# Skip weights loaded as one contiguous row and picked apart by two copies, and a new order of the steps in the output's last four quarters

## The chip, the cores and the metric

The kernel runs on one core of a Trainium2 chip. The metric is device time in microseconds (us) for one execution. Before the change it is 1481.93 us, the median of three runs (1481.75 to 1485.11).

## The reference, cut to what matters

Two layers work on 1024 tokens of width 1024. The first mixes tokens in chunks of 128 by a masked matrix per group (spatial gating); the second is a Mamba-2 scan with 32 heads of 64 channels, whose output gets a skip term. A final RMSNorm closes the program.

```python
h = x
for i in range(2):
    hn = rmsnorm(h, norm_w[i])
    h = h + (spatial_gating_mixer if i == 0 else ssd_mixer)(hn, ...)
return rmsnorm(h, final_norm_w)

# in ssd_mixer: one skip weight per head, d_skip has 32 numbers
y = y_diag + y_off + x * d_skip.reshape(G, J)[..., None]
```

## The kernel before, in words

**Products.** Every large product is a blocked one with seven block products in place of eight. Its float32 operands are split into a high part, a cast on ScalarE (ACT), and a low part, a subtraction on VectorE (DVE); the helper `split` (L111, L112) does this, and `mm3` (L134 to L136) makes three matmuls of the parts. The halves of the weights lie in rotating buffers `wh` and `wl`, three of each. All instructions are written out by hand in program order for each engine; each engine works through its own list in that order and waits where an operand is missing.

**The first layer's wide products.** `head` and then `rest` (L886) compute the gate path `v` for eight groups in two wide blocks, A and B. The object `Wide` has `prep` (ACT cast `wh`, DVE rest `wl`), `mm`, `keep` (ACT copies an accumulator to `u`) and `out`: DVE adds the accumulator and `u` into a tile `vt` (L396) and a DMA stores it in `v_d` (L397). Four buffers of the tag `k2` hold the `vt` tiles. The second block's `C11` is stored through the DMA queue of GpSimd (POOL); the stores around it go through SyncE's queue (SP).

**The mixing matrices.** Among the products of `rest` lie `mix_b`, in which TensorE (PE) transposes the masked matrices `ws` (L869) and ACT copies the result to two tiles `wc` (L871), and `mix_c`, in which PE multiplies `wc` by a matrix of ones (L877) and DVE makes `ab` of it (L882). The `wc` tiles are `k2` tiles too: they take the buffers of the first two `vt` tiles of `C11`, so ACT can write them once the DMAs that store these have landed. Product 6 runs around `mix_b`; L877 stands on PE between products 6 and 7.

**The small constants.** Between `head` and `rest` (L829 to L840) SP loads `dt_bias` and `a_log` into `hv`, and the skip weights into `dsk`: partition p of `dsk` needs, in column c, the weight of head 2c for p below 64 and of head 2c + 1 above. The load does this itself, in two DMAs, each with every second number of `d_skip` as source and 64 partitions as target. `dsk` is first used on DVE at L2024, in the second layer.

**The end.** The second layer's output product, the object `Out` called `bo`, ends with block product 3, cut in four units of 128 tokens (`last_mm`, 24 matmuls each). For a unit, `prep_unit` makes the halves `wh` and `wl` of its operand `ya`; `post(3, i)` adds the accumulator to the residual row `u` on DVE (L1232) and ACT squares it (L1251); `rstd_a` adds the two halves' sums on DVE (L1265) and raises them to the power of -1/2 on POOL (L141); `rstd_b` refines this on DVE (L148, L152, L153); `finish_b` scales the left half of the row on ACT (L2201) and the right half on DVE (L2203) and stores both (L2202, L2204), from SP but for the very last left half, which goes from ACT. The left halves were already multiplied by the final norm's weight (`weigh_left`, L2209). The upper four tiles of 128 tokens, `(1, tt)`, have their norm from `rstd_half` in one go before the last product; the lower four, `(0, tt)`, get theirs one by one as their units end.

Of the kernel before, what the change touches and what calls it, by code (L numbers as in the profile page):

```python
# [8 lines left out]
F32 = mybir.dt.float32  # L9
F32R = mybir.dt.float32r  # L10
AF = mybir.ActivationFunctionType
ALU = mybir.AluOpType
# [3 lines left out]
P = 128  # L16
# [13 lines left out]
def kernel(  # L30
# [21 lines left out]
    nc = tc.nc  # L52
    x = x[0]
    out = out[0]
# [3 lines left out]
    cst = ctx.enter_context(tc.tile_pool(name="cst", bufs=1))  # L58
# [12 lines left out]
    def k2(shape, name, dt=F32):  # L71
        return sb.tile(shape, dt, name=name, tag="k2", bufs=4)
# [755 lines left out]
    with tc.manual_schedule():  # L828
        second = head()  # L829
        hv = cst.tile([P, 4], F32, name="hv")  # L830
        nc.sync.dma_start(out=hv[0:32, 0:1], in_=b_dt_bias[0].rearrange("(h o) -> h o", o=1))
        for q in range(4):
            nc.sync.dma_start(out=hv[q * 32:(q + 1) * 32, 1:2], in_=b_a_log[0].rearrange("(h o) -> h o", o=1))
        dsk = cst.tile([P, 16], F32, name="dsk")
        dskv = b_d_skip[0].rearrange("(c f) -> f c", f=2)
        for f in range(2):
            nc.sync.dma_start(out=dsk[f * 64:(f + 1) * 64, :], in_=dskv[f].partition_broadcast(64))
        nA = hv[:, 2:3]
        nc.scalar.activation(nA, hv[:, 1:2], AF.Exp)
        nc.vector.tensor_scalar(nA, nA, -1.0, None, ALU.mult)  # L840
# [1279 lines left out]
    def accs_b(n):  # L2120
        if n == 1:
# [3 lines left out]
    bo = Out(gd, b_w_out, gscale, lambda t, nb: h1_d[t][:, nb * 512:(nb + 1) * 512], accs_b, False,  # L2125
             (1, 2, 7, 6, 4, 5, 3))
    end = {}
# [68 lines left out]
            if c == 3:  # L2196
                bo.prep_unit(0)

    def finish_b(th, tt, rs):
        l, r = bo.row(th, tt, 0), bo.row(th, tt, 1)  # L2200
        nc.scalar.activation(l, l, AF.Identity, scale=rs)  # L2201
        (nc.scalar if (th, tt) == (0, 3) else nc.sync).dma_start(out=outr[th * 4 + tt][:, 0:512], in_=l)  # L2202
        nc.vector.scalar_tensor_tensor(r, r, rs, end["fnwb"][:, 512:], ALU.mult, ALU.mult)  # L2203
        nc.sync.dma_start(out=outr[th * 4 + tt][:, 512:], in_=r)  # L2204

    def weigh_left(th, t0):
        for tt in range(t0, t0 + 2):
            r = bo.row(th, tt, 0)
            nc.vector.tensor_tensor(out=r, in0=r, in1=end["fnwb"][:, 0:512], op=ALU.mult)  # L2209
# [221 lines left out]
    def into_end():  # L2431
        for n in (2, 7, 6, 4, 5):
            for _ in bo.product(n, hook_b):
                pass
        bo.prep_unit(1)
        weigh_left(1, 2)
        r1 = bo.rstd_half(1)
        for tt in range(4):
            bo.last_mm(tt)
            if 0 < tt < 3:  # L2440
                bo.prep_unit(tt + 1)
            if tt:
                bo.post(3, tt - 1)
                bo.rstd_a(0, tt - 1)
            finish_b(1, tt, r1[:, tt:tt + 1])
            if tt:
                finish_b(0, tt - 1, bo.rstd_b(0, tt - 1))
        bo.post(3, 3)
        bo.rstd_a(0, 3)
        finish_b(0, 3, bo.rstd_b(0, 3))  # L2450

    with tc.manual_schedule():
        scans()
        into_end()
# [28 lines left out]
```

## Time and profile before

| What | us |
|---|---|
| median of three runs | 1481.93 |
| the profiled execution's own time | 1481.93 |
| its span in the profile | 1480.2 |
| PE busy in the span | 1452.0 |
| DVE busy | 1041.8 |
| ACT busy | 784.1 |
| POOL busy | 404.5 |

The profile is of one execution. Its span leaves out 1.73 us of the execution's own time, and that time is the median of the runs. A line of the timeline has the start, the duration, the engine, the line in the code, the operation, what it writes and reads, how often it is repeated and, in brackets, how long the engine had stood idle before it and what ended the wait. PEld is the load of weights into PE, which runs beside matmuls. A busy time of PE is not PE at its peak, so the granted clock, which a table by windows gives as PEclk (1.00 is full), is read with it.

### The profile page before, as it was taken

How to read it: one execution, taken by the hardware profiler on the slowest of the kernel's cores; microseconds unless marked ns; L12 is line 12 of the kernel's file. 1: busy time of each engine (PE TensorE's matmuls, PEld its weight loads, DVE VectorE, ACT ScalarE, POOL GpSimd, SP SyncE). 2: the span in 40 equal slices, each digit the busy share in tenths (PEclk: the TensorE clock that was granted, in tenths of full speed). 3: DMA queues.
4: the chain of work that ended last, by engine and by line, in shares of the span. 5: the costliest groups of instructions: out<-in, count | busy, mean ns of one | idle time of the engine just before them, and what ended most of it. 6: DMA issues, size and time to landing. Idle time of an engine off the chain costs nothing. (4 is left out here: it accounts for less than half of the span.)

```text
span 1480.2 us, 20005 instructions
## 1 busy us (share of the span) xinstructions
PE 1452.0 (98%) x7202; PEld 1196.5 (81%) x7202; DVE 1041.8 (70%) x1713; ACT 784.1 (53%) x1261; POOL 404.5 (27%) x451
## 2 busy tenths in 40 slices
PE   9998999999999999999999999999999999999997
PEld 7786888888888888887788888888888888787875
DVE  7864666776666655678665558767787777788976
ACT  7632333222323445565665646657677766866463
POOL 2101110000000023202122323205676767742221
PEclk9999999999999999999999999999999999999999
DMA  8653423332322999957467988786777566699963
GB/s 287 128 171 91 165 91 120 105 120 94 116 85 78 341 265 252 258 132 175 120 159 169 197 163 162 156 248 158 203 185 201 176 190 141 192 282 282 271 115 114
DMA packets 174549, 257.52 MB, mean 174 GB/s; under 512 B 16513, under 2 KB 98673, under 8 KB 171250
## 3 DMA queue, kind: packets, MB, share of 16 engines
q1 hardware_dynamic: 124128, 171.55, 37.7%
q0 software_dynamic: 42688, 70.79, 24.2%
q10 hardware_dynamic: 7634, 13.90, 2.6%
q8 instruction: 57, 0.93, 0.3%
q14 instruction: 42, 0.34, 0.1%
HBM read 187.19 MB, written 51.18 MB: 161 GB/s over the span
## 5 line engine op out<-in xcount | busy, mean ns | idle before, releaser
L134 PE MATMUL acc<-hh,wh 128*128 128x512 f32 x868 | 339.7, 391 | 0.7 <-ACT u L297 0.7
L136 PE MATMUL acc<-hh,wl 128*128 128x512 f32 x868 | 338.3, 390 | 0.4 <-DVE wl L112 0.3
L135 PE MATMUL acc<-hl,wh 128*128 128x512 f32 x868 | 337.8, 389 | 0.0
L136 PEld LDWEIGHTS acc<-hh,wl 128*128 128x128 f32 x868 | 162.9, 188 | 35.7 <-DVE wl L112 1.6
L134 PEld LDWEIGHTS acc<-hh,wh 128*128 128x128 f32 x868 | 163.1, 188 | 34.3 <-ACT u L297 1.1
L135 PEld LDWEIGHTS acc<-hl,wh 128*128 128x128 f32 x868 | 163.0, 188 | 33.0
L112 DVE TENSOR_TENSOR wl<-wr,wh 128x1024 fp32r<-128x1024 f32 (+1 forms) x81 | 96.2, 1188 | 105.8 <-ACT wh L111 105.6
L111 ACT CAST wh<-wr 128x1024 fp32r<-128x1024 f32 (+1 forms) x97 | 99.3, 1025 | 78.7 <-PE acc L135 58.7
L297 ACT COPY u<-acc 128x512 f32<-128x512 f32 x93 | 53.9, 582 | 148.0 <-PE acc L136 147.9
L134 PE MATMUL ab<-hh,wh 128*128 128x512 f32 x288 | 122.2, 424 | 0.0
L136 PE MATMUL ab<-hh,wl 128*128 128x512 f32 x288 | 113.2, 393 | 0.0
L135 PE MATMUL ab<-hl,wh 128*128 128x512 f32 x288 | 112.5, 391 | 0.6 <-DVE hl L112 0.6
L134 PE MATMUL acc<-wh,hh 128*128 128x512 f32 x216 | 85.6, 396 | 0.3 <-DVE vt L396 0.3
L135 PE MATMUL acc<-wl,hh 128*128 128x512 f32 x216 | 84.3, 390 | 1.0 <-DVE wl L364 1.0
L136 PE MATMUL acc<-wh,hl 128*128 128x512 f32 x216 | 84.1, 389 | 0.0
L976 POOL DMA_DIRECT2D y_d<-y x8 | 4.4, 550 | 287.2 <-DVE y L973 287.2
L1949 ACT ACTIVATE wl<-wl,tk 128x128 f32<-128x128 f32 x256 | 81.6, 392 | 0.3 <-DMA wl<-cs_d 0.2
L1967 DVE TENSOR_TENSOR wl<-wl,cw 128x512 f32<-128x512 f32 x64 | 61.0, 965 | 16.2 <-ACT wl L1951 15.1
L112 DVE TENSOR_TENSOR xl<-ya,xh 128x1024 fp32r<-128x1024 f32 x36 | 44.8, 1243 | 37.6 <-ACT xh L111 32.4
L1162 PE MATMUL bo<-wl,xh 128*128 128x512 f32 x192 | 64.2, 392 | 1.3 <-DVE stats L1253 0.7
L134 PEld LDWEIGHTS ab<-hh,wh 128*128 128x128 f32 x288 | 54.4, 189 | 13.3 <-issue 5.7
L111 ACT CAST xh<-ya 128x1024 fp32r<-128x1024 f32 x36 | 37.7, 1048 | 49.8 <-PE ao L1162 35.0
(331 smaller groups left out, 3236.4 us busy)
## 6 DMA issues: line engine op xcount, KB each, us to landing
wr<-in_a_w_in_dram SPq DMA_DIRECT2D x32, 512.0 KB, 3.6
wl<-cs_d SPq DMA_DIRECT2D x64, 256.0 KB, 5.4
wr<-in_b_w_in_dram SPq DMA_DIRECT2D x30, 512.0 KB, 4.3
wb<-in_a_w_out_dram SPq DMA_DIRECT2D x10, 1024.0 KB
wb<-in_b_w_out_dram SPq DMA_DIRECT2D x10, 1024.0 KB, 9.4
wr<-in_b_w_in_dram SPq DMA_DIRECT2D x36, 256.0 KB, 5.3
wide<-in_a_w_in_dram SPq DMA_DIRECT2D x16, 512.0 KB, 7.3
v<-v_d SPq DMA_DIRECT2D x8, 1024.0 KB
```

Of the source, the lines that this page charges most:

```text
L111: nc.scalar.copy(out=hi, in_=src)
L112: return (eng or nc.vector).tensor_tensor(out=lo, in0=src, in1=hi.bitcast(F32), op=ALU.subtract)
L134: nc.tensor.matmul(out=o, lhsT=l[0], rhs=r[0], start=start, stop=False, **kw)
L135: nc.tensor.matmul(out=o, lhsT=l[0], rhs=r[1], start=False, stop=False, **kw)
L136: nc.tensor.matmul(out=o, lhsT=l[1], rhs=r[0], start=False, stop=stop, **kw)
L297: nc.scalar.copy(out=self.u[n][:, i], in_=a)
L976: store = lambda: nc.gpsimd.dma_start(out=y_d[-1], in_=y)
L1162: nc.tensor.matmul(out=o[i], lhsT=X[x_][:, k, i * P:(i + 1) * P], rhs=Y[y_][:, k, :], start=not more and c == 0 and k == 0 and x_ == y_, s ...
L1949: nc.scalar.activation(wl[:, j, :], wl[:, j, :], AF.Relu, scale=-1.0, bias=tokc(2, c, self.g)[:, j:j + 1])
L1967: V.tensor_tensor(out=wl, in0=wl, in1=self.cw[c][:, 640:768].unsqueeze(1).broadcast_to([P, 4, P]), op=ALU.mult)
```

## The change

The two DMAs that pick every second skip weight become one DMA, which copies the 32 numbers as they lie in memory to each of 128 partitions, and two DVE copies that pick every second column out of that tile into `dsk`. In the output's last four units the same steps are put in another order, and one of them is taken in two: for the very last right half, the multiplication by the final norm's weight is made ahead of the norm, into a tile `left`, and only the scaling by the norm follows.

```diff
+        skip = cst.tile([P, 16, 2], F32, name="skip")
+        nc.sync.dma_start(out=skip.rearrange("p c f -> p (c f)"), in_=b_d_skip[0].partition_broadcast(P))
         dsk = cst.tile([P, 16], F32, name="dsk")
-        dskv = b_d_skip[0].rearrange("(c f) -> f c", f=2)
         for f in range(2):
-            nc.sync.dma_start(out=dsk[f * 64:(f + 1) * 64, :], in_=dskv[f].partition_broadcast(64))
+            nc.vector.tensor_copy(out=dsk[f * 64:(f + 1) * 64, :], in_=skip[f * 64:(f + 1) * 64, :, f])
...
-    def finish_b(th, tt, rs):
+    def finish_b(th, tt, rs, weighed=None):
...
-        nc.vector.scalar_tensor_tensor(r, r, rs, end["fnwb"][:, 512:], ALU.mult, ALU.mult)
+        if weighed is None:
+            nc.vector.scalar_tensor_tensor(r, r, rs, end["fnwb"][:, 512:], ALU.mult, ALU.mult)
+        else:
+            nc.vector.tensor_scalar(r, weighed, rs, None, ALU.mult)
...
-        for tt in range(4):
-            bo.last_mm(tt)
-            if 0 < tt < 3:
-                bo.prep_unit(tt + 1)
-            if tt:
-                bo.post(3, tt - 1)
-                bo.rstd_a(0, tt - 1)
-            finish_b(1, tt, r1[:, tt:tt + 1])
-            if tt:
-                finish_b(0, tt - 1, bo.rstd_b(0, tt - 1))
+        bo.last_mm(0)
+        bo.prep_unit(2)
+        bo.last_mm(1)
+        bo.post(3, 0)
+        bo.rstd_a(0, 0)
+        finish_b(1, 0, r1[:, 0:1])
+        bo.prep_unit(3)
+        finish_b(0, 0, bo.rstd_b(0, 0))
+        bo.last_mm(2)
+        bo.post(3, 1)
+        finish_b(1, 1, r1[:, 1:2])
+        bo.rstd_a(0, 1)
+        finish_b(1, 2, r1[:, 2:3])
+        finish_b(0, 1, bo.rstd_b(0, 1))
+        bo.last_mm(3)
+        bo.post(3, 2)
+        bo.rstd_a(0, 2)
+        finish_b(1, 3, r1[:, 3:4])
+        finish_b(0, 2, bo.rstd_b(0, 2))
         bo.post(3, 3)
+        left = k2([P, 512], "left")
+        nc.vector.tensor_tensor(out=left, in0=bo.row(0, 3, 1), in1=end["fnwb"][:, 512:], op=ALU.mult)
         bo.rstd_a(0, 3)
-        finish_b(0, 3, bo.rstd_b(0, 3))
+        finish_b(0, 3, bo.rstd_b(0, 3), left)
```

In the changed file the lines stand one further down from L838 on; the multiplication of a right half, L2203, is L2205 there, and its store, L2204, is L2208. These are SP's DMAs between `head` and `rest`, before:

```order
L397 DMA v_d_79<-vt 256x1x256
L831 DMA hv<-in_b_dt_bias_dram 32x1
L833 DMA hv<-in_b_a_log_dram 32x1 x4
L837 DMA dsk<-in_b_d_skip_dram 64x16x1 x2
L937 DMA v<-v_d_78 128x2048
```

And the same place on SP with the change:

```order
L397 DMA v_d_79<-vt 256x1x256
L831 DMA hv<-in_b_dt_bias_dram 32x1
L833 DMA hv<-in_b_a_log_dram 32x1 x4
L835 DMA skip<-in_b_d_skip_dram 128x32
L938 DMA v<-v_d_78 128x2048
```

Two DMAs with an innermost step of one number (64 partitions by 16 by 1) became one with rows of 32 numbers. DVE at the same place, where the `vt` tiles of `C11` are made, before:

```order
L396 TENSOR_TENSOR vt<-acc,u 128x512
L404 BN_STATS stats<-vt 128x6
L840 TENSOR_SCALAR hv<-hv 128x1
L404 BN_STATS stats<-vt 128x6
L396 TENSOR_TENSOR vt<-acc,u 128x512
```

And with the change:

```order
L396 TENSOR_TENSOR vt<-acc,u 128x512
L404 BN_STATS stats<-vt 128x6 x2
L838 COPY dsk<-skip 64x16 x2
L841 TENSOR_SCALAR hv<-hv 128x1
L396 TENSOR_TENSOR vt<-acc,u 128x512
```

The two copies, which wait for the new DMA, stand between the second and the third `vt` tile of `C11`. The third place is DVE's list in the last product, from the norm of the upper four tiles (`rh`) to the second unit's addition, before:

```order
L153 TENSOR_TENSOR rh<-rr,ru 128x4
L2203 SCALAR_TENSOR_TENSOR u<-u,rh,fnwb 128x512
L112 TENSOR_TENSOR wl<-ya,wh 128x512 x2
L1232 TENSOR_TENSOR u<-bo,u 128x512
L1265 SCALAR_TENSOR_TENSOR stats<-stats 128x1
L2203 SCALAR_TENSOR_TENSOR u<-u,rh,fnwb 128x512
L148 SCALAR_TENSOR_TENSOR ru<-rr,stats 128x1
L152 TENSOR_SCALAR ru<-ru 128x1
L153 TENSOR_TENSOR stats<-rr,ru 128x1
L2203 SCALAR_TENSOR_TENSOR u<-u,stats,fnwb 128x512
L112 TENSOR_TENSOR wl<-ya,wh 128x512 x2
L1232 TENSOR_TENSOR u<-bo,u 128x512
```

And with the change:

```order
L153 TENSOR_TENSOR rh<-rr,ru 128x4
L112 TENSOR_TENSOR wl<-ya,wh 128x512 x2
L1233 TENSOR_TENSOR u<-bo,u 128x512
L1266 SCALAR_TENSOR_TENSOR stats<-stats 128x1
L2205 SCALAR_TENSOR_TENSOR u<-u,rh,fnwb 128x512
L112 TENSOR_TENSOR wl<-ya,wh 128x512 x2
L148 SCALAR_TENSOR_TENSOR ru<-rr,stats 128x1
L152 TENSOR_SCALAR ru<-ru 128x1
L153 TENSOR_TENSOR stats<-rr,ru 128x1
L2205 SCALAR_TENSOR_TENSOR u<-u,stats,fnwb 128x512
L1233 TENSOR_TENSOR u<-bo,u 128x512
L2205 SCALAR_TENSOR_TENSOR u<-u,rh,fnwb 128x512
```

The operand of unit 2 now comes first and the first upper right half behind the first addition; the operand of unit 3 stands between the sum of unit 0 (L1266) and the refinement of its root (L148); one upper half has moved behind the second addition. On ACT the casts for unit 2 now follow those for unit 1 without an upper left half between them. PE's list and POOL's list are the same in both kernels.

## The prediction

> **What bounds the kernel now.** I read the first part of the page, then the waits of PE, the longest first.
>
> ```profile
> PE 1452.0 (98%) x7202; PEld 1196.5 (81%) x7202; DVE 1041.8 (70%) x1713; ACT 784.1 (53%) x1261; POOL 404.5 (27%) x451
> ...
> PE tp L877 <- ACT wc L871: 6.8, 1, 6.8
> PE nw L451 <- POOL ident masks.py:199: 1.4, 1, 1.4
> ```
>
> PE bounds the kernel: 1452.0 of the span's 1480.2 us, so only 28.2 us are idle. One wait, for the two `wc` tiles, is 6.8 us, and the next longest 1.4. The rest of the idle time must lie at the ends. So I looked at two places: around L877, and behind PE's last matmul. First L877, with PE's and ACT's timelines there and the granted clock in two windows:
>
> ```profile
> 133.16 0.39 PE L136 MATMUL acc<-wh,hl 128*128 128x512 f32 x1
> 140.39 3.73 PE L877 MATMUL tp<-wc,ones 128*128 128x512 f32 x4 [6.84 <-ACT wc L871]
> 144.19 0.40 PE L135 MATMUL acc<-wl,hh 128*128 128x512 f32 x1
> 144.43 0.39 PE L136 MATMUL acc<-wh,hl 128*128 128x512 f32 x1
> ...
> 139.75 1.23 ACT L871 COPY wc<-tp 128x512 f32<-128x512 f32 x2 [20.62 <-DMA v_d<-vt]
> ...
> 136.00:137.00 1.00, 0.00 (x0) 0.00 (x0) 0.00 (x0) 0.00 (x0) 0.00 (x0) 1.00 0.05 0
> 142.40:143.40 1.00, 1.00 (x4) 0.48 (x2) 0.79 (x1) 1.00 (x4) 0.00 (x0) 0.50 0.73 270
> ```
>
> PE waits for ACT, and ACT has waited 20.62 us for the DMA that stores a `vt` tile and so frees the buffer of the first `wc`. The wait costs more than itself: the granted clock (third number from the right) falls from 1.00 to 0.50 during it, and L877 and the matmul behind it still run at half. Why is that store late? Here are the stores from POOL in the stretch from 115 to 160 us, the same line's from 160 to 200, the DMAs of the skip weights, and what the queues moved between 117.2 and 139.2 us:
>
> ```profile
> L397 POOL DMA_DIRECT2D v_d<-vt x4: 690/701/729, 119.6 to 123.8; - x4
> DMA to landing us min/median/max: 17.9/19.1/20.0
> ...
> L397 POOL DMA_DIRECT2D v_d<-vt x12: 682/690/702, 162.7 to 189.8; - x12
> DMA to landing us min/median/max: 2.6/2.7/5.0
> ...
> L837 SPq DMA_DIRECT2D dsk<-in_b_d_skip_dram x2: 672/680/687, 117.4 to 118.1; - x2
> ...
> DMA  1000000000000000000000000000000000004799
> q0 software_dynamic: 186, 0.65, 7.7%
> q1 hardware_dynamic: 2230, 0.01, 4.5%
> hv<-in_b_a_log_dram SPq DMA_DIRECT2D x4, 0.1 KB, 2.1
> ```
>
> The four stores take 18 to 20 us to land, the next twelve of the same size 2.6 to 5.0. In between SP's queue (q1) moves 2230 packets that together hold 0.01 MB, and POOL's queue (q0) moves nothing until slice 37 of 40, which is 137 us. The tiny packets are the skip weights: two DMAs of 64 times 16 single numbers are 2048. They come at 2230 / 22 = 101 per us while the transfer engines are 4.5% busy: some 20 us of making descriptors, not of moving data, from 117.4 to about 138.
>
> The second place is the end. These are DVE's rows around its first and last additions there, and PE's last matmul:
>
> ```profile
> 1455.85 0.75 DVE L2203 SCALAR_TENSOR_TENSOR u<-u,rh,fnwb 128x512 f32<-128x512 f32 x1
> 1457.12 1.30 DVE L112 TENSOR_TENSOR wl<-ya,wh 128x512 fp32r<-128x512 f32 x2 [0.52 <-ACT wh L111]
> 1458.33 0.68 DVE L1232 TENSOR_TENSOR u<-bo,u 128x512 f32<-128x512 f32 x1
> ...
> 1464.24 0.68 DVE L1232 TENSOR_TENSOR u<-bo,u 128x512 f32<-128x512 f32 x1
> 1468.35 0.68 DVE L1232 TENSOR_TENSOR u<-bo,u 128x512 f32<-128x512 f32 x1
> 1471.78 0.75 DVE L2203 SCALAR_TENSOR_TENSOR u<-u,stats,fnwb 128x512 f32<-128x512 f32 x1
> 1472.45 0.68 DVE L1232 TENSOR_TENSOR u<-bo,u 128x512 f32<-128x512 f32 x1
> 1473.98 0.16 DVE L1265 SCALAR_TENSOR_TENSOR stats<-stats 128x1 f32<-128x1 f32 x1 [0.85 <-ACT junk L1251]
> 1474.86 0.22 DVE L148 SCALAR_TENSOR_TENSOR ru<-rr,stats 128x1 f32<-128x1 f32 x1 [0.72 <-POOL rr L141]
> 1475.50 0.75 DVE L2203 SCALAR_TENSOR_TENSOR u<-u,stats,fnwb 128x512 f32<-128x512 f32 x1
> ...
> 1469.86 0.39 PE L136 MATMUL bo<-yh,wl 128*128 128x512 f32 x1
> 1475.49 0.72 ACT L2201 ACTIVATE u<-u,stats 128x512 f32<-128x512 f32 x1 [1.55 <-DVE stats L153]
> ```
>
> PE is done at 1470.25, but DVE adds the last unit only at 1472.45: here DVE's list is late by 2.2 us, and everything behind that addition follows in a chain.
>
> **The change part by part.** *The load.* Two DMAs of 2048 single numbers go; one of 128 rows of 128 bytes comes. At 101 packets per us, 128 packets and a few for completion need about 1.4 us, and a small load lands 2.1 us after its issue (the `hv` row): issued at 117.4, it should be there at about 121. POOL's stores, issued from 119.6 on, then take the 2.6 to 5.0 us of the other twelve; the two that `wc` needs land by 126 at worst.
>
> Then `wc` waits only for its transposes, which stand in PE's list one half product ahead of L877:
>
> ```profile
> 127.06 1.03 PE L869 MATMUL tp<-ident,ws 128*128 128x128 f32 x8
> ...
> 1011.63 0.59 PE L1986 MATMUL os<-cw 128*128 128x256 f32 x2
> 1012.07 0.61 PE L1995 MATMUL os<-xbc,state 128*128 128x128 f32 x4
> ```
>
> They end at 128.1; two copies (1.23) give 129.3. PE comes to L877 at 133.39 (133.16 and one step of 0.23, the distance of the matmuls at 144.19 and 144.43), so 4 us of slack cover the copies. Nothing cools the clock then. What L877 takes at full clock is not in the trace, since it runs once. The nearest row is L1986: two passes over 256 columns in 1012.07 - 1011.63 = 0.44, so a pass over 512 takes 0.44 and L877's four 1.76. The second matmul of product 7 then starts at 133.39 + 1.76 + 0.23 = 135.38 in place of 144.19: 8.8 us earlier. The bounds: 6.8 if L877 gains nothing from the clock; 8.8 is also the upper end, as no step is left to shorten. I take 8.8, since the clock was 1.00 until the wait.
>
> What is late next? DVE's low part for product 7's second half: `keep` behind 133.6, a cast of 1.05, a subtraction of 1.22, so 136.5 against 135.1 plus 24 matmuls, 140.6. The loads of the first layer that follow are issued when their buffers are freed, so they move along with PE, and no wait of PE behind this place is over 1.4 us. I take the whole gain as kept.
>
> The Trainium skill, "DMA: Bandwidth & Descriptors", section "Queues, rings and completion order", speaks against this: each transfer engine takes turns between its queues, packet by packet. By that rule POOL's stores need not wait for the end of SP's tiny packets, their lateness has another cause and stays, and this term would be 0. The trace differs: no q0 data until the tiny packets run out.
>
> *The copies.* DVE gets two copies of 64 by 16 between the second and third `vt` tile of `C11`, at about 121.4 (the row of L840 starts at 121.05). The nearest rows are a copy of 128 by 3 and one of 128 by 256, so 0.16 to 0.42 each, and I take 0.2:
>
> ```profile
> L1709 DVE COPY halo<-acc 128x3 f32<-128x3 f32 x8 | 1.3, 156 | 4.9 <-PE acc L136 4.9
> L2011 DVE COPY state<-os 128x256 f32<-128x256 f32 x8 | 3.3, 415 | 0.7 <-POOL ze L2037 0.7
> 141.97 1.22 DVE L364 TENSOR_TENSOR wl<-wide,wh 128x1024 fp32r<-128x1024 f32 x1 [15.43 <-ACT wh L360]
> ```
>
> DVE stands idle 15.43 us soon after, so this costs nothing. The copies also wait for the load, and behind them stand two `vt` tiles, two subtractions and then the low part for product 7: as long as the load lands by 127 or so, DVE reaches that part before ACT's cast is there.
>
> *The order at the end.* Until the first addition DVE now has only the pair of subtractions for unit 2 (1457.12 to 1458.33, 1.21), whose casts no longer wait for the norm: 1455.85 + 1.21 = 1457.06, 1.27 earlier than 1458.33. The distance to the second addition was 5.91, with the pair for unit 3 behind the scaling. Now the pair lies in the wait for POOL's root. Three rows of ACT give when it can start:
>
> ```profile
> 1456.48 1.12 ACT L111 CAST wh<-ya 128x512 fp32r<-128x512 f32 x2
> 1459.11 0.63 ACT L1251 ACTIVATE junk<-u 128x512 bf16<-128x512 f32 x1 [1.50 <-DVE u L1232]
> 1459.74 0.71 ACT L2201 ACTIVATE u<-u,rh 128x512 f32<-128x512 f32 x1
> ```
>
> After an addition come 0.78 to the square (1458.33 to 1459.11), 0.63 to the upper left half, about as much to the cast, and 0.64 to the subtraction (1456.48 to 1457.12): 2.68. The pair takes 1.21, root and scaling 0.64 (1474.86 to 1475.50) and 0.67 (1471.78 to 1472.45): 5.20, so 0.71 less. The other two distances, 4.11 and 4.10, keep their parts: an upper half before the sum lies within the 0.85 us that DVE waits for the square. The last addition comes at 1472.45 - 1.27 - 0.71 = 1470.47, just behind PE's 1470.25, which is the floor (2.2). From there the chain is the same; `left` (0.68) hides in that 0.85 us. The last right half becomes a multiplication with one tensor, which may take less than the 0.75 of now, but the left half on ACT still takes 0.72 beside it, so I count 0. If the early casts help nothing, 0.7 is left. This term: 2.0, between 0.7 and 2.2.
>
> The sum: 8.8 + 2.0 = 10.8 off the profiled execution, whose own time of 1481.93 is the median too: 1471.1 us.
>
> **The rivals.** *The stores are late for another reason.* They are the first on POOL's queue after a long pause, and the rule above says that queues share. Then only the end gains: 1481.93 - 2.0 = 1479.9. Against it: the twelve later stores land early all the same, and q0's start at 137 meets q1's reckoned end at about 138. Chance 0.09.
>
> *A new wait takes part of it.* `wc` is on time, but ACT or DVE hold product 7 or 4, or a transfer that was covered by the pause is late. Half of the 8.8 would go: 1475.5, with a spread from 1473 to 1478. For it: between L877 and product 4's low part DVE has sixteen small operations of the mixing matrices and two subtractions of 1.2 us, and I know their slack only roughly. Chance 0.11.
>
> *Slower: the new load is cut in single numbers too.* Its 128 by 32 numbers would be 4096 packets, 40 us at 101 per us, landing near 158. DVE's copies wait for it, and with them two `vt` tiles with their statistics, two subtractions and product 7's low part (some 6 us of DVE work): PE would start product 7 at 164 in place of 143, so about 21 - 2.0 = 19 us slower, 1501. It decides from the point where the load lands later than about 139. Against it: its rows are contiguous on both sides. Chance 0.03.
>
> **How the numbers follow.** My forecast has the rest, 0.77. A measurement of this kernel tells about 0.3%, 4.4 us, from no change. Faster by more: 0.77 and most of the second rival, 0.87. Within 0.3%: the first rival and a little of the second, 0.10. Slower: 0.03. The range: the terms' lower bounds give 1481.93 - 6.8 - 0.7 = 1474.4, the upper ones 1470.9; with the second rival, and some 2 us below for what the clock or the final stores may give beyond that, 1469.0 to 1476.5.
>
> **What would show it right or wrong.** Right: no wait at L877, a clock of 1.00 from 130 to 145 us, POOL's four stores landing in 2.6 to 5.0, some 2000 packets fewer on q1, and the last addition some 0.2 us behind PE's last matmul. Wrong: the stores still late with the tiny packets gone, a new wait of PE between 133 and 200 us, DVE idle before its two copies, or a last addition more than 1 us behind PE.

## The result, and the profile after

The changed kernel takes 1470.74 us, the median of five runs (1468.51 to 1472.28), against 1481.93 of before, run beside it (five runs, 1481.41 to 1485.11). The ratio is 0.9919, with a 95% interval from 0.9904 to 0.9933: 11.2 us less, where 10.8 had been predicted (1471.1). The profiled execution of the changed kernel is the slowest of its five: 1472.28, span 1470.6.

The first part of its page, and the waits of PE, the longest first:

```profile
PE 1450.5 (99%) x7202; PEld 1196.8 (81%) x7202; DVE 1043.3 (71%) x1716; ACT 783.9 (53%) x1261; POOL 404.0 (27%) x451
...
PE os L1996 <- DVE state L2014: 1.5, 1, 1.5
PE nw L451 <- POOL ident masks.py:199: 1.4, 1, 1.4
```

The wait for `wc` has left the list, and the longest wait is now 1.5 us. Here are PE's and ACT's timelines at the same place (the lines stand one further down than before), and the granted clock in the two windows that were shown of before:

```profile
133.34 0.40 PE L136 MATMUL acc<-wh,hl 128*128 128x512 f32 x1
133.58 1.88 PE L878 MATMUL tp<-wc,ones 128*128 128x512 f32 x4
134.90 0.79 PE L134 MATMUL acc<-wh,hh 128*128 128x512 f32 x1
135.53 0.40 PE L135 MATMUL acc<-wl,hh 128*128 128x512 f32 x1
...
127.86 1.07 ACT L872 COPY wc<-tp 128x512 f32<-128x512 f32 x2 [8.23 <-PE tp L870]
...
136.00:137.00 1.00, 1.00 (x6) 0.83 (x5) 1.00 (x3) 0.00 (x0) 0.00 (x0) 1.00 0.00 0
142.40:143.40 1.00, 1.00 (x6) 0.84 (x5) 0.96 (x2) 1.00 (x2) 0.00 (x0) 1.00 1.00 414
```

ACT now waits for PE's transposes, no longer for a DMA, and copies `wc` 4.7 us before PE gets there. From the last matmul of product 6 to the second of product 7 it is 135.53 - 133.34 = 2.19 us; before it was 144.19 - 133.16 = 11.03. I call this **the stretch** below; it has become 8.84 us shorter. The clock stays at 1.00. This is the line of POOL's stores (the four of `C11` and four later ones) from 115 to 160 us, and the DMA issues from 117.2 to 139.2 us:

```profile
DMA to landing us min/median/max: 2.6/2.8/5.0
...
v_d<-vt POOLq DMA_DIRECT2D x4, 256.0 KB, 2.6
wcT_d<-wc POOLq DMA_DIRECT2D x2, 256.0 KB, 4.1
skip<-in_b_d_skip_dram SPq DMA_DIRECT2D x1, 16.0 KB, 2.8
```

The four stores of `C11` land in 2.6 to 2.7 us (the 5.0 belongs to a later store), where it had been 18 to 20. At the end, DVE's rows from the first addition to the last right half, and PE's last matmul:

```profile
1450.03 0.68 DVE L1233 TENSOR_TENSOR u<-bo,u 128x512 f32<-128x512 f32 x1
...
1455.20 0.68 DVE L1233 TENSOR_TENSOR u<-bo,u 128x512 f32<-128x512 f32 x1
...
1459.31 0.69 DVE L1233 TENSOR_TENSOR u<-bo,u 128x512 f32<-128x512 f32 x1
...
1463.40 0.69 DVE L1233 TENSOR_TENSOR u<-bo,u 128x512 f32<-128x512 f32 x1
1464.12 0.69 DVE L2463 TENSOR_TENSOR left<-u,fnwb 128x512 f32<-128x512 f32 x1
...
1466.45 0.49 DVE L2207 TENSOR_SCALAR u<-left,stats 128x512 f32<-128x512 f32 x1
...
1462.96 0.39 PE L136 MATMUL bo<-yh,wl 128*128 128x512 f32 x1
```

PE is done at 1463.35, and the last addition follows 0.05 us behind, where it had been 2.20. So the 9.6 us between the two spans come together like this: PE's last matmul is 6.90 earlier (1469.86 - 1462.96), the last addition has moved 2.15 nearer to it, and from there to the end of the span it is 7.20 instead of 7.75. Of the 8.84 us won at the stretch this one pair of executions keeps 6.90 at PE's end; whether that loss belongs to the change is one of the questions below.

### The profile page after: what moved, and what is told of

Its sections match the earlier page's. It is cut to its first block, busy times and chain, and to the rows that moved or that the text cites. A ratio compares the mean times of both kernels' runs of the same rounds, so it can differ in the third digit from the quotient of the medians.

```text
span 1470.6 us, 20006 instructions
## 1 busy us (share of the span) xinstructions
PE 1450.5 (99%) x7202; PEld 1196.8 (81%) x7202; DVE 1043.3 (71%) x1716; ACT 783.9 (53%) x1261; POOL 404.0 (27%) x451
```

## The experiments

Two theories stood at the start. The **theory** is the prediction's: the single numbers of the skip weights hold back POOL's stores, and apart from that the end gains some 2 us of its own. The **rivals**: the stores are late for another reason, and the end gains nothing by itself. The line numbers of an experiment differ by a few from those of before.

### The two parts alone

One kernel has the new load and the old end, the other the old load and the new end (`left` included).

The load alone, against before:

```diff
+        skip = cst.tile([P, 16, 2], F32, name="skip")
+        nc.sync.dma_start(out=skip.rearrange("p c f -> p (c f)"), in_=b_d_skip[0].partition_broadcast(P))
...
-            nc.sync.dma_start(out=dsk[f * 64:(f + 1) * 64, :], in_=dskv[f].partition_broadcast(64))
+            nc.vector.tensor_copy(out=dsk[f * 64:(f + 1) * 64, :], in_=skip[f * 64:(f + 1) * 64, :, f])
```

The order alone, against the changed kernel:

```diff
...
-            nc.vector.tensor_copy(out=dsk[f * 64:(f + 1) * 64, :], in_=skip[f * 64:(f + 1) * 64, :, f])
+            nc.sync.dma_start(out=dsk[f * 64:(f + 1) * 64, :], in_=dskv[f].partition_broadcast(64))
```

> Only the load changes; the order at the end is that of before. Theory (tiny packets hold POOL's stores, wc and PE): no wait at L877's matmul, four stores landing in 2.6 to 5.0 us, 8.8 us less than before, 1473.1 if the scan gives nothing back; 1474.9 if the 1.8 us that the profiled run of after lost in the scan come with every early start. Rival (stores late for another reason): the 6.8 us wait stays, 1481.9. In all cases the last addition lies about 2.2 us behind PE's last matmul.

> Only the order at the end changes, left included; the skip weights come as single numbers. Theory (DVE's list was late by 2.2 us): the last addition falls within 0.3 us of PE's last matmul, 2.0 us less than before by the prediction, 1479.9; 2.5 less, 1479.4, if the 0.55 us between last addition and end is saved too. Rival (the end gains nothing of its own, and the shorter end of after came with the early start): 1481.9. The wait of 6.8 us at L877's line stays in both.

On one chip, with 15 runs of before at 1482.42 us (1480.71 to 1484.49): the load alone took 1473.04 (five runs, 1472.48 to 1473.75), ratio 0.9937 with an interval from 0.9924 to 0.9949, so 7.6 to 11.3 us less. The order alone took 1480.29 (eleven runs, 1477.49 to 1482.80), ratio 0.9983, from 0.9974 to 0.9992, so 1.2 to 3.9 us less. The stretch is 2.19 us with the load alone and 11.17 with the order alone. Here are the last addition and PE's last matmul, first of the load alone, then of the order alone:

```profile
1464.49 0.69 DVE L1233 TENSOR_TENSOR u<-bo,u 128x512 f32<-128x512 f32 x1
...
1461.90 0.39 PE L136 MATMUL bo<-yh,wl 128*128 128x512 f32 x1
```

```profile
1472.46 0.68 DVE L1232 TENSOR_TENSOR u<-bo,u 128x512 f32<-128x512 f32 x1
...
1472.01 0.39 PE L136 MATMUL bo<-yh,wl 128*128 128x512 f32 x1
```

With the old end the addition lies 2.20 us behind PE's end, with the new one 0.06. Added, the medians of the two parts give 9.4 + 2.1 = 11.5 us, where the changed kernel gained 11.2: within the scatter the parts simply add up, and each is worth what the theory gave it. The load alone came to 1473.04, not to 1474.9: the loss between the stretch and the end does not come with every early start.

### The end without `left`

```diff
-        left = k2([P, 512], "left")
-        nc.vector.tensor_tensor(out=left, in0=bo.row(0, 3, 1), in1=end["fnwb"][:, 512:], op=ALU.mult)
...
-        finish_b(0, 3, bo.rstd_b(0, 3), left)
+        finish_b(0, 3, bo.rstd_b(0, 3))
```

> The changed kernel, with the last right half weighed and scaled in one three-operand instruction as before, and no left tile. Theory (that half sets the last store, and its 0.75 us instead of 0.49 is the missing 0.55 us at the end, with the store's distance from the other): from the last addition to the end 7.5 to 7.75 us instead of 7.20, and 0.3 to 0.5 us more than the changed kernel, 1471.2. Rival (the prediction's: ACT's 0.72 us half beside it covers the difference): 7.2 us and the changed kernel's time, 1470.7.

It took 1470.42 us (four runs, 1468.31 to 1472.47), ratio to before 0.9919, from 0.9905 to 0.9932: the changed kernel's own ratio. From last addition to the end of the span it is 7.56 us here, and with `left` it was 7.20 in the changed kernel and 7.64 with the order alone. Over all the profiles of this document that distance is 7.2 to 7.6 us in the seven kernels with `left` (7.5 on average) and 7.5 to 7.9 in the six without it (7.7 on average). So `left` may be worth some 0.2 or 0.3 us, which is no more than its last multiplication is shorter (0.49 us instead of 0.75), but no median shows it, and the rest of the 0.55 us is scatter between executions. The prediction's 0 is right within what the times can tell.

### One step of the end put back

```diff
-        bo.prep_unit(3)
         finish_b(0, 0, bo.rstd_b(0, 0))
+        bo.prep_unit(3)
```

> The changed kernel with one step of the end put back: the pair of subtractions for unit 3 stands behind the scaling again, in front of the second addition, as before; the casts of unit 2 stay ahead of the norm. Theory (the two parts of the end's gain are separate): the first addition keeps its place, 13.3 us ahead of PE's end, the distance to the second grows from 5.17 to about 5.9, and the last addition lies about 0.75 us behind PE's last matmul instead of 0.05; in the time 0.7, less than one run can tell. Rival (the pair only fills a wait, and PE sets the pace of the additions): distances and the 0.05 us stay.

The first, the second and the last addition, and PE's last matmul:

```profile
1447.29 0.68 DVE L1233 TENSOR_TENSOR u<-bo,u 128x512 f32<-128x512 f32 x1
...
1453.20 0.68 DVE L1233 TENSOR_TENSOR u<-bo,u 128x512 f32<-128x512 f32 x1
...
1461.40 0.68 DVE L1233 TENSOR_TENSOR u<-bo,u 128x512 f32<-128x512 f32 x1
...
1460.21 0.39 PE L136 MATMUL bo<-yh,wl 128*128 128x512 f32 x1
```

PE's end is 1460.60. The first addition stands 13.31 us ahead of it (13.32 in the changed kernel, 11.92 before), the distance to the second is 5.91 as before (5.17 in the changed kernel), and the last addition is 0.80 us late. The two parts of the end's gain are separate and have the sizes of the theory. The time, 1470.28 us in a single execution, cannot show 0.7.

### More single numbers

The kernel before, with a third load of the same kind into a tile that nobody reads.

```diff
+        dsk2 = cst.tile([P, 16], F32, name="dsk2")
+        nc.sync.dma_start(out=dsk2[0:64, :], in_=dskv[0].partition_broadcast(64))
```

> The kernel before with a third tiny load of 64 times 16 single numbers into an unused tile, 3072 tiny packets instead of 2048. Theory: at about 101 packets per us they run to about 148, POOL's first stores land 28 to 30 us after their issue, PE waits about 16.9 us instead of 6.8 for wc, and the time is 10 us more, 1492. Rival (the stores are late for another reason, such as the pause of POOL's queue): unchanged, 1481.9.

It took 1481.56 us in a single execution, where 1492 was expected: a miss. PE's wait, what the queues moved from 123 to 137 us and from 143 to 145 us, and the third and the fourth store:

```profile
PE tp L879 <- ACT wc L873: 7.5, 1, 7.5
...
q1 hardware_dynamic: 1504, 0.01, 4.7%
...
q0 software_dynamic: 118, 0.41, 49.7%
q1 hardware_dynamic: 206, 0.00, 5.1%
...
L397 POOL DMA_DIRECT2D v_d<-vt x2: 687/687/687, 122.9 to 124.3; - x2
DMA to landing us min/median/max: 22.6/23.0/23.4
```

Until 137 us POOL's queue (q0) moves nothing, as before. Then its stores move beside the third load's numbers, which go on at 103 per us. So it is not that POOL's queue stands still as long as single numbers pass. The third load was issued from 119.40 to 122.49, the first two stores from 120.14 and 121.51, while it was still being issued. I changed the theory: the stores wait for the numbers that were issued ahead of them. This run bears that out for the first two loads alone. The third and the fourth store were issued behind the whole third load, at 122.94 and 124.32, and yet had landed by 147, while that load landed at 148.7 (119.40 and 29.3). Why they did not wait for its numbers too stays open.

### Half the numbers, and the same numbers later

The first, e5, is the changed kernel with one half of the old load in place of one copy, the second, e8, the kernel before with its two DMAs behind the four stores: a fill of `dsk` on DVE makes SP wait.

```diff
-        for f in range(2):
-            nc.vector.tensor_copy(out=dsk[f * 64:(f + 1) * 64, :], in_=skip[f * 64:(f + 1) * 64, :, f])
+        dskv = b_d_skip[0].rearrange("(c f) -> f c", f=2)
+        nc.vector.tensor_copy(out=dsk[0:64, :], in_=skip[0:64, :, 0])
+        nc.sync.dma_start(out=dsk[64:128, :], in_=dskv[1].partition_broadcast(64))
```

The second, e8, takes these lines out of their old place and puts them in `rest` behind the loop that stores `C11`:

```diff
...
+        nc.vector.memset(dsk, 0.0)
+        dskv = b_d_skip[0].rearrange("(c f) -> f c", f=2)
+        for f in range(2):
+            nc.sync.dma_start(out=dsk[f * 64:(f + 1) * 64, :], in_=dskv[f].partition_broadcast(64))
```

> The changed kernel with half of the old load back: one half of the skip weights comes as 1024 single numbers, the other is copied from the contiguous rows. Theory after e4 (POOL's stores wait for the single numbers that were issued ahead of them, at about 106 per us): the numbers run from 118 to about 128, the first stores move from then on and land some 10 us late, 9 to 11 us after their issue instead of 2.6 to 5.0 or 18 to 20; wc is there by about 131, PE comes at 133.4, so no wait at L877's matmul and the changed kernel's time, 1468.5 to 1472.5. Rival (the hold does not go by the count, any stream of single numbers costs the 18 to 20 us): the 6.8 us wait is back, 1479.5.

> The kernel before with the same 2048 single numbers, issued behind the four stores of C11: the load waits for a fill of dsk on DVE that stands behind the fourth vt tile, at about 124.4. Theory (what was issued ahead of the single numbers does not wait, what comes behind does): the four stores land in 2.6 to 5.0 us, no wait at L877's matmul, 1473.1; the two stores of wcT, issued at about 130 behind them, now land only at about 145, some 15 us instead of 2.4 to 4.1. Rival (the load costs PE its 8.8 us wherever it stands): 1481.9. A second rival (queues share, and the hold came from something else at 119 us): the stores at 130 land in 3 to 8 us.

The half load: 1472.45 us, stretch 2.18. Its stores' line, and ACT's first copy:

```profile
v_d<-vt POOLq DMA_DIRECT2D x4, 256.0 KB, 10.6
...
131.71 0.59 ACT L873 COPY wc<-tp 128x512 f32<-128x512 f32 x1 [12.19 <-DMA v_d<-vt]
```

Half the numbers give 10.6 us instead of 19, and `wc` is just in time. The late load: 1473.73 us, stretch 2.19, with the `C11` stores in front of the numbers and the `wcT_d` stores behind them:

```profile
v_d<-vt POOLq DMA_DIRECT2D x4, 256.0 KB, 2.7
...
wcT_d<-wc POOLq DMA_DIRECT2D x2, 256.0 KB, 18.2
```

The old load, only issued later, costs nothing: the stores ahead of it land in 2.7 us, and those behind it, which now take 18.2, have nobody waiting for them at that time. Both fit the changed theory. (Each of these runs is one execution, as are the next four, so that differences of 2 or 3 us between them show nothing; before took 1483.57 beside e5 to e8, and 1480.82 beside e9 to e11.)

### The stores on another queue

```diff
-            B.out("C11", i, 2, 1, G_)
+            B.out("C11", i, 2, 1, nc.scalar)
```

> The kernel before, single numbers and all, but the four stores of C11 go out through ACT's queue instead of POOL's. Theory A (only POOL's software queue is held): the four land in 2.6 to 5.0 us, no wait at L877's matmul, 1473.1. Theory B (whatever is handed to the transfer engines behind the single numbers waits, on any queue): they land in 18 to 20 us, the wait of 6.8 us stays, 1481.9, or a little more, as ACT now waits for each vt tile.

It took 1482.67 us, stretch 11.08. PE's wait, the four stores, and the only queue that moved anything from 121 to 137 us:

```profile
PE tp L877 <- ACT wc L871: 6.7, 1, 6.7
...
v_d<-vt ACTq DMA_DIRECT2D x4, 256.0 KB, 15.6
...
q1 hardware_dynamic: 1716, 0.01, 4.7%
```

ACT's queue is held just as POOL's is (it moves 949 packets from 138 to 141 us, when the numbers are all but through), so theory B holds for these 2048 numbers: what is issued behind them waits, on either of the queues tried.

### Is it the size, the number, or the place?

What makes the numbers slow was still a reading of the prediction, not a measurement. Three further loads, each added to the changed kernel ahead of the stores, each of 2048 pieces into a tile that nobody reads. In e7 they have 16 bytes and come from 2048 places:

```diff
+        fat = cst.tile([P, 16, 4], F32, name="fat")
+        nc.sync.dma_start(out=fat, in_=xr[0].rearrange("p (c f) -> p c f", f=64)[:, :, 0:4])
```

In e9 they have 4 bytes and come from 2048 places:

```diff
+        far = cst.tile([P, 16], F32, name="far")
+        nc.sync.dma_start(out=far, in_=xr[0].rearrange("p (c f) -> p c f", f=64)[:, :, 0])
```

In e10 they have 16 bytes and all come from the 128 bytes of the skip weights:

```diff
+        near = cst.tile([P, 16, 4], F32, name="near")
+        for q in range(4):
+            nc.sync.dma_start(out=near[:, 4 * q:4 * q + 4, :],
+                              in_=b_d_skip[0].rearrange("(c f) -> c f", f=8)[:, 0:4].partition_broadcast(P))
```

> The changed kernel with a further load ahead of the stores, into a tile that nobody reads: 2048 runs of 16 bytes out of the rows of x, so as many pieces as the old skip load, each four times as large. Theory (the number of pieces sets the hold): q1 passes them at about 106 per us until 138, the stores land in 18 to 20 us, the wait at L877's matmul is back, 1479.5. Rival (it is the single 4-byte element, not the count): the pieces pass several times as fast, the stores land by 126 to 128 and the time is the changed kernel's, 1470.7.

> The changed kernel with a further load ahead of the stores, into a tile that nobody reads: 2048 single numbers again, but from 2048 different places, every 64th number of 128 rows of x. Theory S (a piece of 4 bytes is what is slow): q1 passes them at about 106 per us, POOL's four stores land in 18 to 20 us, the wait at L877's matmul is back, 1479.5. Theory P (it is the reading of one place in memory again and again, as the skip weights are 32 numbers that every partition reads): they pass at some 1000 per us like the 16-byte pieces of e7, the stores land in 2.6 to 5.0 us and the time is the changed kernel's, 1468.5 to 1472.5.

> The changed kernel with four further loads ahead of the stores, into a tile that nobody reads: 2048 pieces of 16 bytes, as in e7, but all out of the 128 bytes of the skip weights, each quarter of 512 by a DMA of its own. Theory P (one place read again and again): about 106 pieces per us, as for single numbers, 19 us, the stores land in 15 to 20 us, the wait at L877's matmul is back, 1479.5. Theory S (pieces of 4 bytes are slow, of 16 are not): about 1000 per us as in e7, the stores land in 2.6 to 5.0 us, 1468.5 to 1472.5.

Here is q1 in the same window, 120 to 122 us, of before and of e7, e9 and e10 in this order; the first number counts packets:

```profile
q1 hardware_dynamic: 213, 0.00, 4.7%
```

```profile
q1 hardware_dynamic: 2126, 0.04, 59.9%
```

```profile
q1 hardware_dynamic: 2040, 0.01, 57.5%
```

```profile
q1 hardware_dynamic: 213, 0.00, 4.7%
```

Single numbers from different places pass at 1020 per us, and pieces of 16 bytes from one place at 106, just like the old skip load. So neither the size nor the number of the pieces makes the load slow. What the slow loads share is that all partitions read the same 128 bytes. They also share the tensor: every slow load reads `d_skip` and every fast one `x`. A load that reads one place of `x` again and again was not run, so that the reads are slow because of where `d_skip` lies is not excluded. The times go along: e7 took 1470.72 us and e9 1471.19, with a stretch of 2.19 and 2.18 and `C11` stores that land in 2.6 to 3.3 and 2.6 to 3.5; e10 took 1477.93, stretch 11.80, and its waits and stores show the old picture:

```profile
PE tp L882 <- ACT wc L876: 8.0, 1, 8.0
...
DMA to landing us min/median/max: 18.9/20.3/21.1
```

Theory S falls, and theory P holds with that reservation. (e10 is 1.6 us faster than expected, less than the 3.8 us between the slowest and the fastest of the changed kernel's own five runs.)

## Why the prediction was right, point by point

**The load, 8.8 us.** The size and the path are as predicted. The stores land on time, `wc` waits for PE alone, the clock stays at 1.00. From L877's start to the second matmul of product 7 it is 1.95 us (135.53 - 133.58), where 1.76 + 0.23 = 1.99 was reckoned, and PE reaches that matmul at 135.53 (predicted 135.38, with PE 0.18 us later already ahead of L877). The stretch gives 8.84, and the load alone 7.6 to 11.3 in the time.

**The reason given for it was wrong in one step.** "Some 20 us of making descriptors, not of moving data" took the number of tiny packets for the cause. e9 passes as many just as tiny ones in 2 us. What took 20 us is 2048 reads out of the same 128 bytes, at 106 per us with 4 bytes as with 16. (The prediction's 101 per us divides all 2230 packets of the queue by 22 us; in the middle, where only single numbers pass, it is 106.) The change removes 2048 of these reads and adds 128, each of 128 bytes. They too pass at about 100 per us, which is why the reckoning of 1.4 us for the new load came out right. That was luck: the prediction carried the rate over because it took it for a rate of packets of any kind, and the new load happens to read the same place. Where a load reads that place as often in larger pieces, as the one of e10 does, the wait is back.

**The first rival** (the stores late for another reason) fell with e1 and e5. The rule behind it, that of the Trainium skill, "DMA: Bandwidth & Descriptors", section "Queues, rings and completion order", that each transfer engine takes turns between its queues, agrees with 143 to 145 us of e4, where both queues move side by side. It does not describe the 17 us from the first store's issue, at 120.1, to 137 in which POOL's queue moved no packet, nor the same time in e6 for ACT's.

**The second rival** (a new wait takes half of it): there is none between 133 and 200 us. In the profiled pair PE has lost 1.9 of the 8.84 us by its last matmul: 0.18 ahead of the stretch (133.34 against 133.16), the rest behind it, where the longest wait is 1.5 us, in the second layer's scan (L1996 in the first fence). It is no price of the early start. With the load alone PE reaches the second matmul of product 7 7.10 us earlier than before (137.09 against 144.19) and its last matmul 7.96 us earlier (1461.90 against 1469.86), so there nothing is lost behind the stretch, and the median shows the load's full worth. The profile of e3, which differs from the changed kernel in the last right half alone, ends its matmuls 4.38 us earlier (1458.58 against 1462.96). So the 1.9 us are scatter between executions; what makes it in the scan was not followed up.

**The third rival** (the new load is cut in single numbers): one DMA, 128 packets, 2.8 us to landing.

**The copies** took 0.49 us together at 121.53, without a wait, where 0.2 each was reckoned, and cost nothing.

**The end, 2.0 us.** The last addition moved 2.15 us nearer to PE's end; alone, this part gave 1.2 to 3.9 in the time. Of its two terms the first was 1.40 (1.27 predicted: 13.32 - 11.92 ahead of PE's end), the second 0.74 (0.71 predicted: 5.91 - 5.17), and e11 separated them. The last addition lies 0.05 us behind PE where "some 0.2" was expected.

**`left` at 0** is right within what the times can tell: e3 has the changed kernel's ratio. The 2 us that the range has below for "what the clock or the final stores may give" have no row behind them, and no run showed a gain of that kind.

## What to carry to other kernels

Look at where a broadcast load reads before looking at how small its pieces are: here every further read of the same 128 bytes cost 9.4 ns, 2048 of them 19 us, and one contiguous row per partition with a picking copy on an idle engine cut them to 128. Such a load was paid for by the transfers issued behind it, on other queues too, so it belongs behind those that somebody waits for (e8 lost nothing with the old load, issued 8 us later). At the end of a kernel, count how far the last step of the second engine lies behind the last step of the first: here it was 2.20 us, and the new order won 2.15 of it.

## What the runs showed of the hardware that was not expected

**One place in memory.** 16 bytes or 4, the reads of the 128 bytes of `d_skip` pass at 106 per us (213 in 2 us) while the transfer engines are 4.7% busy; from 2048 places in `x` it is over 1000 per us. Another tensor's one place was not tried, nor how far apart two places must be: in e7 and e9 they lie 256 bytes apart and more.

**Order between queues.** Stores issued behind these reads on POOL's or ACT's queue moved nothing until the reads were all but through (before, POOL's queue moves its first packets between 137 and 138 us, and the last 21 numbers pass between 138 and 139). Those issued ahead were not touched (2.7 us in e8). e4 does not fit: two of its stores were issued behind the third load and yet moved beside it.

**The start.** The same 32 transposes at the start of PE's list take different times from execution to execution. Here is their row from before, and then from the kernel without `left`, each with the window from 12 to 13 us:

```profile
10.62 5.55 PE L460 MATMUL tp<-both,weighed 128*128 128x128 f32 x32 [0.55 <-DVE both L447]
...
12.00:13.00 1.00, 1.00 (x7) 1.00 (x6) 1.00 (x3) 0.26 (x1) 0.00 (x0) 1.00 1.04 387
```

```profile
10.62 3.89 PE L460 MATMUL tp<-both,weighed 128*128 128x128 f32 x32 [0.55 <-DVE both L447]
...
12.00:13.00 1.00, 1.00 (x11) 1.00 (x10) 1.00 (x3) 1.00 (x2) 0.00 (x0) 1.00 1.06 412
```

In the same microsecond the view counts 7 transposes in before and 11 in the other. The clock of 1.00 that it gives for both is no measurement in before: the trace's first record of a granted clock, 1.00, lies at 14.24 us there, and the view counts the time without a record as full. In e3 the first record lies at 9.99 us, ahead of the transposes. In before they start 0.21 us apart up to 14.2 us and 0.11 us apart from then on; in e3 it is 0.11 but for two gaps. So PE runs them at about half its pace until the full clock is granted, and that moment differs between executions. The row goes along in all profiles: 3.89 to 3.90 us in e1, e3, e10 and e11, with first records from 9.99 to 10.51 us; 5.86 in the changed kernel's profile (14.88); 6.52, the longest, in e2's (16.29).

This moves PE by up to 2.6 us at the start of an execution, more than the whole gain of the end, but it does not simply pass on to the time. e1's profile has the short start and is still the slowest of its five: there PE waits 2.1 us for a DVE subtraction (L364) up to 50.27 us, and behind it the clock is 0.66 in the mean from 50 to 55 us. Such differences add to the scatter that hides the gain of the end in single executions.
